# A hybrid decoder trunk on one core: half of the memory's values computed before the output projection, the memory's norm weight moved into the weights' split, other latencies in the order of work

## The chip, the cores and the metric

The kernel runs on one NeuronCore of a Trainium2 chip. The metric is the device time of one execution in microseconds (us). Three runs of the kernel before gave a median of 1250.59 us (1248.96 to 1250.6).

The engines and their short names in the profile: PE (TensorE, matmuls; PEld is its weight loads), ACT (ScalarE), DVE (VectorE), POOL (GpSimd), SP (SyncE, which issues nearly all DMAs here). Each takes its instructions in one fixed order. PE writes into PSUM; ACT and DVE carry results from there to SBUF.

## The reference, cut to what matters

Two layers, 256 tokens, width 1024, all in float32. Each layer is a half-step feed-forward block, a mixer, a cross-attention on 256 memory tokens, and a second half-step feed-forward block:

```
x = x + 0.5 * swiglu(rms_norm(x, ffn1_norm[l]), ...)
x = x + hybrid_mixer(rms_norm(x, mix_norm[l]), w_in[l], ..., w_out[l])
x = x + memory_cross_attention(rms_norm(x, cross_norm[l]), rms_norm(mem, mem_norm[l]),
                               cross_wq[l], cross_wk[l], cross_wv[l], cross_wo[l])
x = x + 0.5 * swiglu(rms_norm(x, ffn2_norm[l]), ...)
...
def memory_cross_attention(h, m, wq, wk, wv, wo):
    q = (h @ wq).reshape(B, S, CROSS_HEADS, CROSS_DH)
    k = (m @ wk).reshape(B, M, CROSS_HEADS, CROSS_DH)
    v = (m @ wv).reshape(B, M, CROSS_HEADS, CROSS_DH)
    ...
```

The keys `m @ wk` and the values `m @ wv` need only the memory, so they can be computed at any time before the attention. `rms_norm(m, w)` is `m / rms(m) * w`, so `rms_norm(m, w) @ W` is `(m / rms(m)) @ (diag(w) W)`: the norm weight may be multiplied into the rows of `W` instead.

The mixer has two groups of heads: HGRN2, a scan over time with a decay (here done as a tree of seven levels), and FoX, causal softmax attention with a forget gate.

## The kernel before, in words

**Products.** Each float32 product is three matmuls on rounded parts: an operand is split into `hi` and `lo`, and `mm3` issues hi·hi, hi·lo and lo·hi (lines L432, L433, L434). Weights come from HBM in slabs of 1 MB (four row blocks of 128 by 512 columns, or two by 1024), in the order of a list `plan`. A slab lands in one of three buffers `raw`; `split_k` makes `whi` (ACT, L140) and `wlo` (DVE, L141), in pieces of 128x1024 with seven buffers each. Where a norm weight is folded into a weight, `split_k` works per row block of 128x512, with a multiplication by a column: ACT L144 and DVE L145. Before the change only the very first feed-forward block does that.

Two forms of product: `xstat` keeps tokens as stationary operand and streams 512 weight columns (matmuls of 128x512), `wstat` keeps weight columns and streams 256 tokens (128x256). Sums go to `acc`, four PSUM tiles in turn; a fifth product waits until the oldest tile is read out. `put_split` (L359 on ACT, then L360 on DVE) does that.

**The order of work** is set by a planner, `drive`: the trunk and the side tasks ("lanes") are generators, which hand over estimated times. A lane yields `(LAT_...,)`, the time that its ACT and DVE work is assumed to take, and until that is over the trunk's matmuls are issued. Within ACT and DVE a scheduler places the instructions, so their order can differ from the code's.

**The mixer** (`mixer`): `xstat` for the scan's values and gate, `wstat` for its forget gates and queries; then the side tasks start: `hgrn` (the scan: `qf`, `kk`, `tots` on DVE, `al` on PE for each level, `ax` and `ho` at its end, `hot` transposes), `memory_task` (loads the memory, L340 squares on ACT, L343 times norm weight and L347 times 1/rms on DVE, then transposes to the features `mf`), `fox_gates`, and two `fox_lane`s of two head pairs each (`fox_stack` makes `fqs` and `fks`; `fs` are the scores, `fpt` the transposed weights, `fpv` the outputs). The trunk meanwhile computes `fq`, `fk`, `fv` (the FoX projections) and the memory's keys `kc` (`wstat` on `mf`, two halves). Then `rows_to_residual` does the output projection: its first matmuls take all four `acc` tiles, and its inputs `oT` come from both groups. The norm of the new residual (`norm_task`) runs beside its end.

**The cross-attention** (`cross`) begins with both halves of the memory's values (`xstat` on `mf`, 48 matmuls of 128x512 each; read out to `vch`, `vcl`), which cover the norm; then queries, scores, and so on.

Of the kernel before, what the change touches and what calls it, by code (L numbers as in the profile page):

```python
# [8 lines left out]
F32 = mybir.dt.float32  # L9
# [8 lines left out]
P = 128  # L18
# [13 lines left out]
HP = 100  # L32
LA_D, LA_S = 3, 1
LAT_NORM, LAT_X = 5.5, 6.5
LAT_LVL, LAT_AX, LAT_HN = 3.0, 1.0, 3.5
LAT_FS, LAT_FT, LAT_CQ, LAT_CS, LAT_CT = 6.0, 2.5, 2.6, 5.6, 3.0
LAT_Q, LAT_G1, LAT_G2, LAT_M = 5.0, 9.0, 2.0, 18.0
LAT_HT = 2.4
LAT_FK = 5.0

OFF_Q, OFF_F, OFF_I, OFF_G = 0, 512, 1024, 1536
OFF_FQ, OFF_FK, OFF_FV = 2048, 2560, 3072
# [3 lines left out]
def hymba_kernel(  # L46
# [43 lines left out]
    def add_cols(w, l, c0, cw, scaled=False):  # L90
        for k0 in range(0, KT, 4):
            plan.append((kview(w, l, c0, cw, k0, 4), 4, cw, k0 if scaled else None))
# [5 lines left out]
    def add_ffn(g, u, d, l, scaled=False):  # L98
        for c0, cw in FCH:
            add_cols(g, l, c0, cw, scaled)  # L100
            add_cols(u, l, c0, cw, scaled)
        add_rows(d, l, FT)

    for l in range(DEPTH):
        add_ffn(ffn1_g, ffn1_u, ffn1_d, l, l == 0)
        for o in (OFF_I, OFF_G, OFF_F, OFF_Q):
            add_cols(w_in, l, o, 512)
        add_cols(w_in, l, OFF_FV + 260, 260)
        add_cols(w_in, l, OFF_FQ, 512)
        add_cols(w_in, l, OFF_FK, 512)  # L110
        add_cols(w_in, l, OFF_FV, 260)
        add_cols(c_wk, l, 0, 512)
        add_cols(c_wk, l, 512, 512)
        add_rows(w_out, l, KT)
        for w in (c_wv, c_wq):
            for c0 in (0, 512):
                add_cols(w, l, c0, 512)
        add_rows(c_wo, l, KT)
        add_ffn(ffn2_g, ffn2_u, ffn2_d, l)

    raws = []
# [13 lines left out]

    def split_k(i, sl, k, hi, lo):

        k0 = plan[i][3]
        if k0 is None:
            nc.scalar.copy(out=hi, in_=sl)  # L140
            nc.vector.tensor_tensor(out=lo, in0=sl, in1=hi.bitcast(F32), op=ALU.subtract)  # L141
        else:
            g = g0[:, k0 + k:k0 + k + 1]
            nc.scalar.mul(hi, sl, g)  # L144
            nc.vector.scalar_tensor_tensor(out=lo, in0=sl, scalar=g, in1=hi.bitcast(F32), op0=ALU.mult,  # L145
                                           op1=ALU.subtract)
# [77 lines left out]
    with in_order():  # L224
        warm_up(14)
        nc.tensor.transpose(g0t[:, 0:8], grow, ident[0:8, 0:8])
        nc.vector.tensor_copy(out=g0, in_=g0t[:, 0:8])
        warm_up(12)
    neghalf = cp.tile([P, 4], F32, name="neghalf")
    nc.vector.memset(neghalf, -0.5)  # L230

    lbr = cp.tile([8, P], F32, name="lbr")

    def consts_mixer():
        it = s4([P, P], I32, "it")
# [626 lines left out]
    def fox_stack(pr, fq, fk, L_, R_, oh):  # L862


        qs = s4([P, 2, 2, S], F32R, "fqs")
        ks = s4([P, 2, 2, S], F32R, "fks")
        for sub in range(2):
            h = 2 * pr + sub
            own = slice(sub * 64, sub * 64 + 64)
            oth = slice(64 - sub * 64, 128 - sub * 64)  # L870
            qv, kv = fq[own, pr, :], fk[own, pr, :]
            nc.scalar.copy(out=qs[own, :, sub, :], in_=qv.unsqueeze(1).to_broadcast([64, 2, S]))  # L872
            nc.scalar.copy(out=ks[own, 0, sub, :], in_=kv)  # L873
# [3 lines left out]
            nc.vector.tensor_tensor(out=ks[own, 1, sub, :], in0=kv, in1=ks[own, 0, sub, :].bitcast(F32),  # L877
                                    op=ALU.subtract)
            nc.vector.tensor_scalar(out=qs[oth, 1, sub, :], in0=L_[oth], scalar1=oh[oth, h:h + 1],
                                    scalar2=None, op0=ALU.mult)  # L880
            nc.gpsimd.tensor_copy(out=ks[oth, 1, sub, :], in_=R_[oth])
# [55 lines left out]
    def mixer(cur, l, consts, nxt_w):  # L937
# [104 lines left out]
    def cross(cur, kc, mf, nxt_w):  # L1042
        f = cur.f
        oT = Feat("cT")
        evs = [Event() for _ in range(4)]
        vc = []

        def head(c, b, qh, ql):
            yield (LAT_CQ,)
# [33 lines left out]
                      po.rearrange("p (k t) -> p k t", k=2))  # L1083
            evs[2 * c + b].fire(1.8)

        for c in range(2):
            vh = s4([P, NT, 512], F32R, "vch")
            vl = s4([P, NT, 512], F32R, "vcl")
            ps = []
            yield from xstat(mf, 512, ps)  # L1090
            for t in range(NT):
                put_split(vh[:, t, :], vl[:, t, :], ps[t])
# [21 lines left out]
    def trunk():  # L1114
        cur = First()
        consts = []

        def early():
            yield (20.0,)
            yield from lower_bounds()  # L1120
            consts.extend(consts_mixer())

        spawn(early())
        for l in range(DEPTH):
            nxt = yield from ffn(cur, mix_norm[l], first=l == 0)
            nxt, kc, mf = yield from mixer(nxt, l, consts, cross_norm[l])
            nxt = yield from cross(nxt, kc, mf, ffn2_norm[l])
# [31 lines left out]
```

## Time and profile before

| | |
|---|---|
| median of three runs | 1250.59 us |
| profiled execution, its time | 1250.42 us |
| its span (first to last instruction) | 1248.6 us |
| mean granted TensorE clock | 0.997 |
| PE busy | 1231.8 us, 99% of the span |
| DVE busy | 767.1 us, 61% |
| ACT busy | 641.2 us, 51% |
| POOL busy | 38.7 us, 3% |
| HBM read | 218.32 MB, 176 GB/s over the span |

The profiled execution took 1.8 us more than its span and lies 0.2 us under the median of the runs. Matmuls overlap in the records (a 128x256 one is recorded as 0.28 us and the next starts 0.12 us after it), so a full PE is read from the starts. The mixer of the first layer lies at about 200 to 356 us, that of the second about 615 us later.

### The profile page before, as it was taken

The numbers are of one execution on the slowest core, as the hardware profiler recorded it, in microseconds if no ns is written. First come the engines' busy times: TensorE is split into PE (matmuls) and PEld (weight loads), VectorE is DVE, ScalarE is ACT, GpSimd is POOL, SyncE is SP. The second block draws the span as 40 slices with busy tenths as digits, with TensorE's granted clock in tenths as the row PEclk, the third lists the DMA queues.
The fourth block names the chain that finished last, engine by engine and source line by source line (L and its number), as shares of the span: only waits on it lengthen the run. The fifth ranks groups of instructions, "written<-read, shape, count | busy, mean of one in ns | idle before, by whom it ended". The sixth has DMA issues, their size and how long they took to land.

```text
span 1248.6 us, 21619 instructions
## 1 busy us (share of the span) xinstructions
PE 1231.8 (99%) x9074; PEld 1126.3 (90%) x9074; DVE 767.1 (61%) x1163; ACT 641.2 (51%) x986; POOL 38.7 (3%) x52
## 2 busy tenths in 40 slices
PE   9999999999999999999999999999999999999997
PEld 7999888989889889998889998889997898999986
DVE  7756547597775675464474464476786766545643
ACT  7555535657754454444354353366585655544532
POOL 0000000002000000000000000000020000000000
PEclk9999999999999999999999999999999999999999
DMA  9555754643453374565474555465442633555640
GB/s 319 178 180 170 239 199 157 219 158 113 169 187 134 102 253 146 192 204 201 135 253 138 200 202 202 135 220 189 147 157 102 248 117 124 177 195 169 236 169 34
DMA packets 100514, 220.76 MB, mean 177 GB/s; under 512 B 4145, under 2 KB 16705, under 8 KB 100417
## 3 DMA queue, kind: packets, MB, share of 16 engines
q1 hardware_dynamic: 100256, 219.11, 51.8%
q8 instruction: 71, 1.16, 0.4%
q10 hardware_dynamic: 160, 0.27, 0.1%
q14 instruction: 27, 0.21, 0.1%
HBM read 218.32 MB, written 1.05 MB: 176 GB/s over the span
## 4 chain that ended last, share of the span: by engine, by line
PE 91%; ACT 5%; DVE 3%; issue 1%; POOL 1%; DMA 0%; POOLq 0%; SPq 0%; ACTq 0%; DVEq 0%
PE acc L432 28%; PE acc L433 28%; PE acc L434 28%; PE pt L353 1%; ACT whi L140 1%; ACT pp L856 1%; ACT fqs L872 1%; DVE wlo L141 1%; PE al L732 1%; ACT fks L874 1%; ACT fks L873 0%; POOL mrs L334 0%; PE cpo L433 0%; DVE mem L343 0%; PE cs L433 0%
## 5 line engine op out<-in xcount | busy, mean ns | idle before, releaser
L141 DVE TENSOR_TENSOR wlo<-raw,whi 128x1024 fp32r<-128x1024 f32 (+1 forms) x356 | 426.3, 1222 | 287.0 <-ACT whi L140 286.0
L140 ACT CAST whi<-raw 128x1024 fp32r<-128x1024 f32 (+1 forms) x356 | 362.8, 1048 | 303.3 <-PE acc L434 152.4
L432 PE MATMUL acc<-xfh,whi 128*128 128x256 f32 x1536 | 434.5, 283 | 0.0
L434 PE MATMUL acc<-xfh,wlo 128*128 128x256 f32 x1536 | 431.0, 281 | 1.9 <-DVE wlo L141 1.9
L433 PE MATMUL acc<-xfl,whi 128*128 128x256 f32 x1536 | 432.0, 281 | 0.0
L434 PEld LDWEIGHTS acc<-xfh,wlo 128*128 128x128 f32 x1536 | 290.2, 189 | 2.1 <-DVE wlo L141 2.1
L433 PEld LDWEIGHTS acc<-xfl,whi 128*128 128x128 f32 x1536 | 290.9, 189 | 0.4
L432 PEld LDWEIGHTS acc<-xfh,whi 128*128 128x128 f32 x1536 | 289.5, 188 | 0.9
L432 PE MATMUL acc<-whi,hth 128*128 128x512 f32 (+1 forms) x352 | 136.4, 388 | 0.0
L433 PE MATMUL acc<-wlo,hth 128*128 128x512 f32 (+1 forms) x352 | 136.3, 387 | 0.0
L434 PE MATMUL acc<-whi,htl 128*128 128x512 f32 (+1 forms) x352 | 135.8, 386 | 0.0
L432 PE MATMUL acc<-whi,xfh 128*128 128x512 f32 (+1 forms) x256 | 95.0, 371 | 0.4 <-ACT xfh L359 0.4
L433 PE MATMUL acc<-wlo,xfh 128*128 128x512 f32 (+1 forms) x256 | 94.0, 367 | 0.0
L434 PE MATMUL acc<-whi,xfl 128*128 128x512 f32 (+1 forms) x256 | 93.6, 366 | 0.1
L434 PEld LDWEIGHTS acc<-whi,htl 128*128 128x128 f32 x352 | 66.2, 188 | 14.5
L432 PEld LDWEIGHTS acc<-whi,hth 128*128 128x128 f32 x352 | 66.1, 188 | 14.4
L433 PEld LDWEIGHTS acc<-wlo,hth 128*128 128x128 f32 x352 | 66.1, 188 | 14.0
L145 DVE SCALAR_TENSOR_TENSOR wlo<-raw,g,whi 128x512 fp32r<-128x512 f32 (+1 forms) x96 | 61.9, 702 | 26.0 <-PE acc L434 18.5
L144 ACT ACTIVATE whi<-raw,g 128x512 fp32r<-128x512 f32 (+1 forms) x96 | 58.2, 678 | 24.5 <-PE acc L433 16.7
L434 PEld LDWEIGHTS acc<-whi,xfl 128*128 128x128 f32 x256 | 48.1, 188 | 8.9 <-DVE xfl L360 0.4
L432 PEld LDWEIGHTS acc<-whi,xfh 128*128 128x128 f32 x256 | 48.1, 188 | 8.8 <-ACT xfh L359 0.6
L433 PEld LDWEIGHTS acc<-wlo,xfh 128*128 128x128 f32 x256 | 48.2, 188 | 8.5 <-DVE wlo L145 0.4
(255 smaller groups left out, 1424.4 us busy)
## 6 DMA issues: line engine op xcount, KB each, us to landing
raw<-in_ffn_w_down_dram SPq DMA_DIRECT2D x44, 1024.0 KB, 4.9
raw<-in_ffn_w_up_dram SPq DMA_DIRECT2D x40, 1024.0 KB, 5.1
raw<-in_ffn_w_gate_dram SPq DMA_DIRECT2D x38, 1024.0 KB, 5.2
raw<-in_w_in_dram SPq DMA_DIRECT2D x24, 1024.0 KB, 5.3
raw<-in_cross_wk_dram SPq DMA_DIRECT2D x8, 1024.0 KB, 5.0
raw<-in_w_out_dram SPq DMA_DIRECT2D x8, 1024.0 KB, 4.8
raw<-in_cross_wv_dram SPq DMA_DIRECT2D x8, 1024.0 KB, 5.3
raw<-in_cross_wq_dram SPq DMA_DIRECT2D x8, 1024.0 KB, 5.6
```

Of the source, the lines that this page charges most:

```text
L140: nc.scalar.copy(out=hi, in_=sl)
L141: nc.vector.tensor_tensor(out=lo, in0=sl, in1=hi.bitcast(F32), op=ALU.subtract)
L144: nc.scalar.mul(hi, sl, g)
L145: nc.vector.scalar_tensor_tensor(out=lo, in0=sl, scalar=g, in1=hi.bitcast(F32), op0=ALU.mult, op1=ALU.subtract)
L353: nc.tensor.transpose(pt[:, j * P:(j + 1) * P], hn[:, kt * P:(kt + 1) * P], ident)
L432: nc.tensor.matmul(ps, lhsT=lh, rhs=rh, start=start, stop=False)
L433: nc.tensor.matmul(ps, lhsT=lh, rhs=rl, start=False, stop=False)
L434: nc.tensor.matmul(ps, lhsT=ll, rhs=rh, start=False, stop=stop)
L732: nc.tensor.matmul(ps[s0:s0 + hb, c0:c0 + hb], lhsT=k[:, h, a:a + hb], rhs=rhs[:, h, a + step:a + step + hb], start=True, stop=True)
L856: nc.scalar.activation(dst, src, AF.Exp, bias=nmx[:, t:t + 1], scale=scale, accum_out=sms[:, t:t + 1])
L872: nc.scalar.copy(out=qs[own, :, sub, :], in_=qv.unsqueeze(1).to_broadcast([64, 2, S]))
L874: nc.scalar.copy(out=ks[oth, 0, sub, :], in_=kv)
```

## The change

Four things change.

1. The first half of the memory's values is computed by a new `memory_values`, called in `mixer` between the keys and the output projection; `cross` computes the second half alone. The slabs in `plan` follow: the first half of `c_wv` comes before `w_out`.
2. The memory's norm weight is no longer multiplied into the memory. It is loaded once for both layers together with `hgrn_lb`, transposed to columns `gcols["mem"]`, and folded into `c_wk` and `c_wv` by the split. The 1/rms is applied by one ACT instruction for each half of the tokens.
3. The assumed latencies of the lanes are longer.
4. In `fox_stack` the POOL copy of `R_` is issued first for each head instead of last.

```diff
-LAT_LVL, LAT_AX, LAT_HN = 3.0, 1.0, 3.5
-LAT_FS, LAT_FT, LAT_CQ, LAT_CS, LAT_CT = 6.0, 2.5, 2.6, 5.6, 3.0
+LAT_LVL, LAT_AX, LAT_HN = 4.0, 1.5, 4.0
+LAT_FS, LAT_FT, LAT_CQ, LAT_CS, LAT_CT = 6.5, 3.5, 2.6, 5.6, 3.0
-LAT_FK = 5.0
+LAT_FK = 6.5
...
-        add_cols(c_wk, l, 0, 512)
-        add_cols(c_wk, l, 512, 512)
+        of_mem = ("mem", 8 * l)
+        add_cols(c_wk, l, 0, 512, of_mem)
+        add_cols(c_wk, l, 512, 512, of_mem)
+        add_cols(c_wv, l, 0, 512, of_mem)
         add_rows(w_out, l, KT)
-        for w in (c_wv, c_wq):
-            for c0 in (0, 512):
-                add_cols(w, l, c0, 512)
+        add_cols(c_wv, l, 512, 512, of_mem)
+        for c0 in (0, 512):
+            add_cols(c_wq, l, c0, 512)
...
-            g = g0[:, k0 + k:k0 + k + 1]
+            g = gcols[gk[0]][:, gk[1] + k:gk[1] + k + 1]
             nc.scalar.mul(hi, sl, g)
...
-        nc.sync.dma_start(out=lbr, in_=hgrn_lb.rearrange("d (h p) -> (d h) p", p=P))
+        nc.sync.dma_start(out=lbr[0:8], in_=hgrn_lb.rearrange("d (h p) -> (d h) p", p=P))
+        nc.sync.dma_start(out=lbr[8:24], in_=mem_norm.rearrange("d (k p) -> (d k) p", p=P))
...
+        gcols["mem"] = small(16, "gmem", bufs=1)
+        nc.vector.tensor_copy(out=gcols["mem"], in_=pt[:, 8:24])
...
             qv, kv = fq[own, pr, :], fk[own, pr, :]
+            nc.gpsimd.tensor_copy(out=ks[oth, 1, sub, :], in_=R_[oth])
...
-            nc.gpsimd.tensor_copy(out=ks[oth, 1, sub, :], in_=R_[oth])
...
-        wmem = load_norm(mem_norm[l])
...
+        vc = []
+        yield from memory_values(mf, vc)
         nxt = Next(nxt_w, lat=LAT_X)
...
                 square(jk, mt, ss, j)
-                gain(mt, mt, wn, j)
             rs = small(1, "mrs")
             inv_rms(ss, rs)
-            apply_norm(mt, rs)
+            nc.scalar.mul(mt, mt, rs)
...
+    def memory_values(mf, vc):
+        ps = []
+        yield from xstat(mf, 512, ps)
+        vh = s4([P, NT, 512], F32R, "vch")
+        vl = s4([P, NT, 512], F32R, "vcl")
+        for t in range(NT):
+            put_split(vh[:, t, :], vl[:, t, :], ps[t])
+        vc.append((vh, vl))
...
-        for c in range(2):
-            vh = s4([P, NT, 512], F32R, "vch")
-            ...
-            vc.append((vh, vl))
+        yield from memory_values(mf, vc)
         yield cur.ev[0]
         yield cur.ev[1]
```

Three places of the order are shown, in the first layer; the second has the same. In the names the number behind the underscore tells tiles of one kind apart. The first is DVE where the scan starts, at about 250 us of the profile before. `mem` rows are the memory's norm, `qf`, `kk` and `tots` the scan, `wlo_2712` (before) and `wlo_2707` (now) the last quarter of the `fq` weights. Before:

```order
L343 TENSOR_TENSOR mem_2555<-mem_2555,wn_2096 128x512
L333 SCALAR_TENSOR_TENSOR ms_2564<-mss_2557 128x1
L723 TENSOR_TENSOR qf_2624<-hq_2404,fg_2272 128x1024
L347 TENSOR_SCALAR mem_2555<-mem_2555,mrs_2563 128x512 x2
L759 TENSOR_TENSOR tots_2660<-fg_2272 128x512
L737 TENSOR_TENSOR Ac_2623<-ad_2626,eye 128x256
L759 TENSOR_TENSOR tots_2660<-tots_2660 128x256
...
L753 TENSOR_TENSOR qf_2624<-qf_2624,fg_2272 128x512
L755 TENSOR_TENSOR kk_2273<-kk_2273,fg_2272 128x512
L766 COPY_PREDICATED Ac_2623<-masks,al_2661 128x256
L141 TENSOR_TENSOR wlo_2712<-raw_2525,whi_2711 128x1024
```

Now:

```order
L340 SCALAR_TENSOR_TENSOR ms_2549<-mss_2544 128x1
L730 TENSOR_TENSOR qf_2619<-hq_2405,fg_2273 128x1024
L766 TENSOR_TENSOR tots_2655<-fg_2273 128x512
L766 TENSOR_TENSOR tots_2655<-tots_2655 128x256
L340 SCALAR_TENSOR_TENSOR ms_2560<-mss_2555 128x1
L766 TENSOR_TENSOR tots_2655<-tots_2655 128x128
...
L144 TENSOR_TENSOR wlo_2707<-raw_2526,whi_2706 128x1024
L990 TENSOR_TENSOR zb_2523<-acc_2524,fb_2097 128x8
...
L760 TENSOR_TENSOR qf_2619<-qf_2619,fg_2273 128x512
L762 TENSOR_TENSOR kk_2274<-kk_2274,fg_2273 128x512
```

The memory's products are gone from this stretch, and the weights' piece has moved from behind the first level of the scan (`qf`, `kk`) to ahead of it. On PE the second level of `al` now stands 39 matmuls of `fq` behind the first, where it was cut in two after 20 and 30.

The second is ACT at the end of the mixer, behind the softmax of the last FoX pairs. `kc_3310` and `kc_3247` are the keys' last half, read out of the fourth `acc` tile; `ppT` are the transposed softmax weights. Before:

```order
L856 ACTIVATE pp_3752,fsm_3758<-pp_3752,fnm_3756 128x256
L140 CAST whi_3818<-raw_3550 128x1024
L140 CAST whi_3890<-raw_3560 128x1024
L359 CAST kc_3310<-acc_3683 128x512
L140 CAST whi_3894<-raw_3560 128x1024
L140 CAST whi_3900<-raw_3812 128x1024
L915 COPY ppT_3838<-fpt_3834 128x384
```

Now:

```order
L863 ACTIVATE pp_3770,fsm_3776<-pp_3770,fnm_3774 128x256
L147 ACTIVATE whi_3831<-raw_3569,gmem_599 128x512 x2
L366 CAST kc_3247<-acc_3698 128x512
L143 CAST whi_3887<-raw_3583 128x1024
L143 CAST whi_3891<-raw_3583 128x1024
L143 CAST whi_3951<-raw_3823 128x1024
L922 COPY ppT_3853<-fpt_3849 128x384
```

The read-out of the keys is two short multiplications behind the softmax instead of two long casts; on PE what follows the keys is now 48 matmuls of the memory's values, in two tiles of `acc` that are long free, and the output projection behind them.

The third is DVE where the first FoX softmax starts, at about 304 us of the profile before. The `ISA` rows find the largest score of each query, and `fnm` is the first number that ACT's exponentials wait for; `hss`, `AX` and `oh` are the scan's output norm. Before:

```order
L901 ISA pp_3418,fmx_3419<-fs_3413,cmask 128x128
...
L901 ISA pp_3436,fmx_3437<-fs_3431,cmask 128x128
L901 ISA fmx_3437 128x1
L905 TENSOR_SCALAR fnm_3422<-fmx_3419 128x2
L901 ISA pp_3436,fmx_3437<-fs_3431,cmask 128x256
```

Now:

```order
L806 TENSOR_SCALAR hss_3354<-hss_3354 128x4
L810 SCALAR_TENSOR_TENSOR AX_3330<-ho_3349,hrs_3360,gw_2100 128x128 x4
L908 ISA pp_3393,fmx_3394<-fs_3388,cmask 128x128
...
L806 TENSOR_SCALAR hss_3376<-hss_3376 128x4
L908 ISA pp_3411,fmx_3412<-fs_3406,cmask 128x128
...
L810 SCALAR_TENSOR_TENSOR oh_3375<-ho_3366,hrs_3382,gw_2100 128x128 x4
L912 TENSOR_SCALAR fnm_3397<-fmx_3394 128x2
```

Before, the scan's norm was over when the first scores came; now the two share DVE.

More of the change, by code (lines that the diff above doesn't have):

```diff
@@ L88, in kview, with add_cols @@
         return w[l, k0 * P:(k0 + nk) * P, c0:c0 + cw].rearrange("(k p) c -> p k c", p=P)
-    def add_cols(w, l, c0, cw, scaled=False):
+    def add_cols(w, l, c0, cw, scaled=None):
         for k0 in range(0, KT, 4):
-            plan.append((kview(w, l, c0, cw, k0, 4), 4, cw, k0 if scaled else None))
+            plan.append((kview(w, l, c0, cw, k0, 4), 4, cw, (scaled[0], scaled[1] + k0) if scaled else None))
     def add_rows(w, l, nkt):
@@ L96, in add_rows, with add_ffn @@
             plan.append((kview(w, l, 0, D, k0, 2), 2, D, None))
-    def add_ffn(g, u, d, l, scaled=False):
+    def add_ffn(g, u, d, l, scaled=None):
         for c0, cw in FCH:
@@ L104, in hymba_kernel @@
     for l in range(DEPTH):
-        add_ffn(ffn1_g, ffn1_u, ffn1_d, l, l == 0)
+        add_ffn(ffn1_g, ffn1_u, ffn1_d, l, ("first", 0) if l == 0 else None)
         for o in (OFF_I, OFF_G, OFF_F, OFF_Q):
@@ L122, in hymba_kernel @@
     pieces = []
+    gcols = {}
     taken = [0]
@@ L136, in split_k @@
     def split_k(i, sl, k, hi, lo):
-        k0 = plan[i][3]
-        if k0 is None:
+        gk = plan[i][3]
+        if gk is None:
             nc.scalar.copy(out=hi, in_=sl)
@@ L227, in hymba_kernel @@
         nc.vector.tensor_copy(out=g0, in_=g0t[:, 0:8])
+        gcols["first"] = g0
         warm_up(12)
@@ L230, in hymba_kernel @@
     nc.vector.memset(neghalf, -0.5)
-    lbr = cp.tile([8, P], F32, name="lbr")
+    lbr = cp.tile([24, P], F32, name="lbr")
     def consts_mixer():
@@ L298, in lower_bounds @@
     def lower_bounds():
-        nc.sync.dma_start(out=lbr, in_=hgrn_lb.rearrange("d (h p) -> (d h) p", p=P))
+        nc.sync.dma_start(out=lbr[0:8], in_=hgrn_lb.rearrange("d (h p) -> (d h) p", p=P))
+        nc.sync.dma_start(out=lbr[8:24], in_=mem_norm.rearrange("d (k p) -> (d k) p", p=P))
         yield (6.0,)
         pt = smp("lbt")
-        nc.tensor.transpose(pt[:, 0:8], lbr, ident[0:8, 0:8])
+        nc.tensor.transpose(pt[:, 0:24], lbr, ident[0:24, 0:24])
         yield 0.1
+        gcols["mem"] = small(16, "gmem", bufs=1)
+        nc.vector.tensor_copy(out=gcols["mem"], in_=pt[:, 8:24])
         a = small(8, "lba")
@@ L977, in mixer @@
         mf = Feat("mf")
-        spawn(memory_task(l, wmem, mf, ev_m))
+        spawn(memory_task(mf, ev_m))
         fv = s4([P, NT, 512], F32, "fv")
@@ L1014, in mixer, with memory_task @@
         yield from rows_to_residual(act, KT, 1.0, TAIL, nxt, lambda kt: ev_h if kt < 4 else ev_p[kt - 4])
-        return nxt, kc, mf
-    def memory_task(l, wn, mf, ev):
+        return nxt, kc, vc, mf
+    def memory_task(mf, ev):
         mf.alloc(0)
@@ L1039, in memory_task, with cross @@
         ev.fire(1.6)
-    def cross(cur, kc, mf, nxt_w):
+    def memory_values(mf, vc):
[6 more added lines that the diff above has]
+        vc.append((vh, vl))
+    def cross(cur, kc, vc, mf, nxt_w):
         f = cur.f
@@ L1045, in cross @@
         evs = [Event() for _ in range(4)]
-        vc = []
         def head(c, b, qh, ql):
@@ L1084, in head @@
             evs[2 * c + b].fire(1.8)
-        for c in range(2):
-            vh = s4([P, NT, 512], F32R, "vch")
[L1088 to L1092, printed above, removed]
-            vc.append((vh, vl))
+        yield from memory_values(mf, vc)
         yield cur.ev[0]
@@ L1125, in trunk @@
             nxt = yield from ffn(cur, mix_norm[l], first=l == 0)
-            nxt, kc, mf = yield from mixer(nxt, l, consts, cross_norm[l])
-            nxt = yield from cross(nxt, kc, mf, ffn2_norm[l])
+            nxt, kc, vc, mf = yield from mixer(nxt, l, consts, cross_norm[l])
+            nxt = yield from cross(nxt, kc, vc, mf, ffn2_norm[l])
             cur = yield from ffn(nxt, ffn1_norm[l + 1] if l + 1 < DEPTH else final_norm, l + 1 == DEPTH)
```

## The prediction

> **What bounds the kernel now.** I read the page's busy times first, then PE's list of waits, then the rows around each wait, and last the busy times by stretch.
>
> ```profile
> PE 1231.8 (99%) x9074; PEld 1126.3 (90%) x9074; DVE 767.1 (61%) x1163; ACT 641.2 (51%) x986; POOL 38.7 (3%) x52
> PE acc L432 <- DVE kc L360: 2.9, 2, 1.5
> PE acc L434 <- DVE wlo L141: 1.9, 2, 1.0
> ...
> PE al L732 <- DVE kk L755: 0.8, 2, 0.6
> PE fpv L925 <- ACT ppT L915: 0.7, 2, 0.4
> PE fs L894 <- DVE fks L877: 0.6, 4, 0.2
> ```
>
> PE is the bound, and what is left to gain is small: the five waits that lie in the mixer (`kc`, `wlo`, `kk`, `ppT`, `fks`) come to 2.9 + 1.9 + 0.8 + 0.7 + 0.6 = 6.9 us over both layers. What else the list has lies almost all at the start of the kernel and stays. The change takes no matmul away and adds none of weight, so it can only act on these waits, or make new ones. Where a new one could come is told by the stretches of the first mixer (columns: window; its length; busy us, with counts, of PE, PEld, DVE, ACT, POOL; clock; DMA share; GB/s):
>
> ```profile
> 262.00:282.00 20.00, 20.00 (x369) 18.88 (x367) 16.86 (x30) 12.21 (x20) 0.00 (x0) 1.00 0.55 183
> 282.00:297.00 15.00, 15.00 (x130) 14.99 (x129) 10.32 (x19) 10.05 (x28) 4.69 (x7) 1.00 0.39 142
> 297.00:316.00 19.00, 18.62 (x164) 18.04 (x163) 16.21 (x51) 17.75 (x42) 2.34 (x4) 1.00 0.27 92
> 316.00:333.00 17.00, 15.24 (x112) 14.15 (x112) 15.86 (x52) 14.61 (x39) 0.00 (x0) 1.00 0.29 96
> ```
>
> From 297 to 333 us, where both FoX lanes run beside the keys, ACT is busy for 32.4 of 36 us and DVE for 32.1. There is little cover: what an instruction waits for there depends on its place in the queue.
>
> **Part by part. First, the keys' read-out** (the largest wait). These are PE's rows at the start of the output projection, in which `fpt` is a lane's transposes, and what ACT and DVE did before:
>
> ```profile
> 330.18 0.82 PE L912 MATMUL fpt<-ident,pp 128*128 128x128 f32 x6
> 332.44 0.51 PE L432 MATMUL acc<-whi,oTh 128*128 128x512 f32 x1 [1.45 <-DVE kc L360]
> 333.24 0.82 PE L912 MATMUL fpt<-ident,pp 128*128 128x128 f32 x6
> 333.81 0.47 PE L432 MATMUL acc<-whi,oTh 128*128 128x512 f32 x1
> ...
> 328.36 1.99 ACT L140 CAST whi<-raw 128x1024 fp32r<-128x1024 f32 x2
> 329.43 2.36 DVE L141 TENSOR_TENSOR wlo<-raw,whi 128x1024 fp32r<-128x1024 f32 x2 [0.19 <-ACT whi L140]
> 331.71 0.68 DVE L360 TENSOR_TENSOR kc<-acc,kc 128x512 fp32r<-128x512 f32 x1
> ```
>
> The keys' last product needed 1.99 + 0.6 us on ACT and 2.36 + 0.68 on DVE before its PSUM tile came free; the projection's fourth tile waited for it. The same six transposes without a wait are followed after 333.81 - 333.24 = 0.57 us, here after 2.26, so PE lost 1.7 us, 3.4 in both layers (the list, which counts from the modelled end of the matmul, has 2.9). In the new order 48 matmuls of 128x512 come between, in tiles read out long before. At 0.23 us each (the starts of the rows at 366.98 and 367.21, shown below) they give 11 us of cover: gain 3.4. What is late next are the values' own two tiles, which the projection takes as its third and fourth: needed six and nine matmuls (1.4 and 2.1 us) behind the values' end, and ready, with an ACT copy of 0.6 and a DVE subtraction of 0.68 each, about 0.7 and 1.4 us behind it, if no long cast stands ahead; the last cast ahead waits for a weights' buffer that comes free 2.8 us before the end. I cost this at nothing.
>
> **Second, the scan's start.** PE's rows, one stretch of each layer:
>
> ```profile
> 255.98 0.28 PE L433 MATMUL acc<-xfl,whi 128*128 128x256 f32 x1
> 256.43 0.50 PE L732 MATMUL al<-qf,kk 128*32 128x32 f32 x34 [0.17 <-DVE kk L755]
> 257.89 0.39 PE L434 MATMUL acc<-xfh,wlo 128*128 128x256 f32 x1 [0.96 <-DVE wlo L141]
> ...
> 870.02 0.28 PE L433 MATMUL acc<-xfl,whi 128*128 128x256 f32 x1
> 870.91 0.50 PE L732 MATMUL al<-qf,kk 128*32 128x32 f32 x34 [0.62 <-DVE kk L755]
> 872.38 0.39 PE L434 MATMUL acc<-xfh,wlo 128*128 128x256 f32 x1 [0.96 <-DVE wlo L141]
> ...
> L343 DVE TENSOR_TENSOR mem<-mem,wn 128x512 f32<-128x512 f32 x8 | 5.4, 683 | 0.0
> L347 DVE TENSOR_SCALAR mem<-mem,mrs 128x512 f32<-128x512 f32 x8 | 3.5, 484 | 1.8 <-POOL mrs L334 1.8
> L334 POOL TENSOR_TENSOR mrs<-ms,neghalf 128x1 f32<-128x1 f32 x4 | 4.8, 1196 | 88.7 <-DVE ms L333 88.7
> ```
>
> A matmul and half a level of `al` take 0.12 + 0.5 us; the rows show 1.91 and 2.36, a loss of 1.3 + 1.7 = 3.0 us. Two edits meet here. The memory's products leave DVE: per layer 4 x 0.683 + 4 x 0.484 = 4.7 us, and 0.9 of waiting for POOL. And the order puts the weights' piece ahead of the scan's first level, and 39 matmuls (4.7 us) between the levels. The new DVE queue, from the end of the previous `wlo` at 248.0: `qf` 1.2, `tots` 1.9, then the piece 1.2, so done by about 253 us, while PE wants it at about 255.9. On ACT the two new multiplications of 128x1024 wait for POOL's `mrs` (1.2 us), and the cast `whi_2706` stands behind the first: about 252. The margin is nearly 3 us, and I count the whole 3.0 as gained. The price of such a multiplication is not in the trace; it lies between 1.05 (the cast of that size) and 1.28 us (two scaled pieces, below).
>
> **Third, the two small waits.** `LAT_FT` puts 24 matmuls instead of 15 between `fpt` and `fpv` (2.9 instead of 1.8 us), and in ACT's queue the `ppT` copies stand ahead of the casts; `LAT_FK` puts 51 instead of 36 matmuls before the second `fs`, 1.8 us more for a wait of 0.3 per layer. Gain 0.7 + 0.6 = 1.3, by the list. The POOL copy issued first matters little: it reads `R_` alone.
>
> Together 3.4 + 3.0 + 1.3 = 7.7 us.
>
> **Fourth, what the scaled split costs.** One slab in each form, from the first feed-forward block:
>
> ```profile
> 44.93 2.57 ACT L144 ACTIVATE whi<-raw,g 128x512 fp32r<-128x512 f32 x4 [2.82 <-PE acc L433]
> 45.69 2.74 DVE L145 SCALAR_TENSOR_TENSOR wlo<-raw,g,whi 128x512 fp32r<-128x512 f32 x4 [0.81 <-ACT whi L144]
> L872 ACT CAST fqs<-fq 64x512 fp32r<-64x512 f32 x16 | 10.0, 622 | 0.3
> L873 ACT CAST fks<-fk 64x256 fp32r<-64x256 f32 x16 | 6.5, 404 | 0.0
> ```
>
> Against 1.99 and 2.36 us for the plain form, a slab costs ACT 0.58 and DVE 0.38 us more; with eight slabs a layer that is 4.6 and 3.0 us. PE pays only where a queue is late. The tightest place I find is the scan's last product `ho`: its operand `AX` is copied by ACT behind 12 scaled pieces (7.7 us), nine FoX copies (3 x 0.62 + 6 x 0.40 = 4.3) and six copies out of PSUM or into `A` (some 3 us, an estimate from the 0.40 to 0.62 of copies of like size). With four copies into `A` ahead (1.6) and about 2 us until they can start, that is some 19 us from the fifth level on, while PE covers it with 132 matmuls and three small groups, 132 x 0.12 + 2.5 plus a tenth or two for each change of shape: 19. That is nothing to spare; I take 0 here, and the bounds are 0 and 1 us per layer.
>
> **Fifth, two waits that the new order makes.**
>
> ```profile
> 293.98 1.12 DVE L803 SCALAR_TENSOR_TENSOR oh<-ho,hrs,gw 128x128 f32<-128x128 f32 x4 [1.13 <-POOL hrs L801]
> 304.09 0.28 PE L432 MATMUL acc<-mfh,whi 128*128 128x256 f32 x1
> 304.21 0.28 PE L433 MATMUL acc<-mfl,whi 128*128 128x256 f32 x1
> 310.59 0.55 DVE L860 TENSOR_SCALAR pp<-pp,frc 128x128 f32<-128x128 f32 x2
> 365.88 1.03 PE L353 MATMUL pt<-ident,hn 128*128 128x128 f32 x8
> 366.98 0.40 PE L433 MATMUL acc<-wlo,mfh 128*128 128x512 f32 x1
> 367.21 0.40 PE L434 MATMUL acc<-whi,mfl 128*128 128x512 f32 x1
> 367.71 1.28 DVE L360 TENSOR_TENSOR xfl<-pt,xfh 128x512 fp32r<-128x512 f32 x2
> ```
>
> Matmuls of 128x256 start 0.12 us apart, those of 128x512 0.23. The first softmax took 311.14 - 304.09 = 7.05 us from where PE leaves the scores to the end of DVE's last product. In the new order the scan's norm shares DVE with it: four products (1.1 us) and a wait for POOL (1.1) stand ahead of the first `fnm`. PE covers 48 matmuls and three groups of transposes, 5.8 + 2 = 7.8 us. With 1.1 us added the last transposes wait about 0.4 us per layer (bounds 0 and 1.5, with POOL's wait paid in full). At the start of the cross-attention the second set of `xf` is ready at 367.71 + 0.68 = 368.4; of the matmuls of 128x512 behind the transposes (366.98 is the second), six are left, so the first matmul on `xf` would start at 366.98 + 5 x 0.23 = 368.1 and the second, which reads this set, at 368.2: 0.2 us per layer (bounds 0 and 0.7, one read-out more). Together 0.8 + 0.4 = 1.2 us.
>
> The rest is small: one DMA of 16 short rows and a copy of 16 columns more, two loads of a norm weight fewer, on queues that nothing here waits for.
>
> **The sum.** 1250.4 - 7.7 + 1.2 = 1243.9 us, against the profiled execution's own time, which lies 0.2 us under the median.
>
> **Rivals.** (a) The waits come back in part: ACT and DVE, full for 36 us, pass their 4.6 and 3.0 us on where I took 0. With 1 us at `ho` and 0.75 more at the softmax in each layer, 3.5 us are lost again: 1247.4.
>
> (b) Nothing in sum: the lanes' slack only moves from wait to wait, as the waits of 0.2 to 0.6 us at many places suggest; 1249 to 1252. Against it: the largest, `kc`, is removed by 11 us of cover.
>
> (c) Slower: ACT becomes the bound at `ho`. Each microsecond that the `AX` copy is late beyond the 19 us above stops PE for one, in both layers. It decides from (6.5 + 2.5) / 2 = 4.5 us per layer on: the scaled pieces would have to take 1.0 us instead of 0.64, or a slab's DMA to hold ACT that long. Time then 1253 or more. Against it: the first block's rows show four pieces in 2.57 us.
>
> (d) POOL's copies against the splits. Beside DVE's `wlo` a copy took much longer than alone:
>
> ```profile
> L881 POOL CAST fks<-R x16: 393/399/1349, 294.0 to 919.7; 64x256 fp32r<-64x256 f32 x16
> ```
>
> If each of the eight copies per layer, now issued among the scan's and the splits' work, held DVE for its 0.4 us and PE paid half, 2 x 8 x 0.4 / 2 = 3.2 us come back: 1247.1. I doubt it, since nothing waited for POOL there. The Trainium skill, "SBUF — State Buffer", section "Who interferes with whom", has a rule that speaks for it: a DVE instruction with two SBUF inputs contends with a GpSimd instruction that reads SBUF, and the later one is blocked in full. By that rule the trace's 1.35 us copies are blocked ones, which agrees; whether DVE was held in turn, no row here shows. By the rule the sum would be 1247.1, by the rows 1243.9.
>
> **Chances.** My sum 0.60 (its own range 1241.3 to 1246.5: with no new wait and what PE loses beyond the list at the small waits too, or with the upper bounds at one place); (a) 0.13; (d) 0.05; (b) 0.14; (c) 0.08. A measurement of this kernel tells a change from none beyond about 0.2%, 2.5 us, so under 1248.1 us counts as faster: 0.78; same 0.14; slower 0.08. The range takes in (a) and (d) and part of (b): 1241 to 1249.5.
>
> **What would show it.** In the list of PE's waits `kc` and the splits' `wlo` should be gone from the mixer, `ppT` and `fks` nearly; a wait of `fpt` for DVE `pp`, and one of `acc` for `xfl`, a few tenths each, should be there. `ho` waiting for ACT `AX` shows (a) or (c). I would be wrong if the values' tiles `vcl` came late, since nothing but DVE's order covers them, or if the memory's multiplication on ACT, held up by `mrs`, made the casts behind it late for `fq`.

## The result and the profile after

The changed kernel takes 1242.62 us in the median of four runs (1242.16 to 1242.67), the kernel before 1249.89 us on the same chip; the ratio is 0.9941, 95% interval 0.9928 to 0.9953. The forecast of 1243.9 us and its sign hold. The runs of the kernels without part 2, the one before among them, fall into two groups some 1.4 us apart (22 of 83 in the upper; of the kernel before two of each here, near 1249.1 and 1250.5 us, the profiled one in the upper), which leaves about 0.7 us of doubt in the gain of 7.3. The profiled execution's span went from 1248.6 to 1240.8 us, by 7.8.

First the page's busy times, then PE's list of waits, of the changed kernel (us in total, times, longest). Between the two kernels the line numbers shift by 7 where the code is the same:

```profile
PE 1227.8 (99%) x9074; PEld 1122.9 (90%) x9074; DVE 767.1 (62%) x1180; ACT 653.6 (53%) x1022; POOL 36.9 (3%) x52
PE fs L901 <- DVE AX L810: 2.1, 2, 1.1
PE warm L223 <- POOL ident masks.py:199: 1.4, 1, 1.4
PE pt L501 <- DVE hn L494: 1.0, 1, 1.0
PE acc L439 <- ACT xfh L366: 0.6, 1, 0.6
PE al L739 <- issue: 0.5, 1, 0.5
PE fpt L919 <- DVE oTl L367: 0.3, 2, 0.2
```

All five waits that the prediction wanted gone are gone: `kc`, the splits' `wlo`, `kk`, `ppT`, `fks`. In their place stands a wait that it did not have: the scores `fs` for DVE's `AX`, once in each layer. The rows around it, PE and then DVE, in the first layer:

```profile
297.82 1.17 PE L901 MATMUL fs<-fks,fqs 128*128 128x128 f32 x8
300.04 1.28 PE L901 MATMUL fs<-fks,fqs 128*128 128x128 f32 x8 [1.06 <-DVE AX L810]
301.16 0.28 PE L439 MATMUL acc<-mfh,whi 128*128 128x256 f32 x1
297.49 0.17 DVE L806 TENSOR_SCALAR hss<-hss 128x4 f32<-128x4 f32 x1 [1.25 <-ACT AX L804]
298.86 1.12 DVE L810 SCALAR_TENSOR_TENSOR AX<-ho,hrs,gw 128x128 f32<-128x128 f32 x4 [1.20 <-POOL hrs L808]
299.90 0.28 DVE L908 CUSTOM_DVE_ANT_0 pp<-fs,cmask 128x128 f32<-128x128 f32 x1
301.75 1.13 DVE L810 SCALAR_TENSOR_TENSOR oh<-ho,hrs,gw 128x128 f32<-128x128 f32 x4 [0.93 <-POOL hrs L808]
```

The second eight score products start 1.12 us before the next row, the first eight 2.22 before the second: PE lost 1.1 us, 2.2 in both layers. `fs` computes nothing from `AX`. What the two share is PSUM: everything that isn't `acc` takes one of four tiles (`pss`, `bufs=4`). `ho` takes two of them, the first two `fs` tiles the other two (eight of the sixteen products), and the third `fs` tile is that of the first `ho`, which `AX<-ho` is still reading. The tiles are not taken strictly in turn. If they were, the fourth `fs` tile would be that of the second `ho`; but `oh<-ho` reads that one only from 301.75 us on, and all sixteen products have begun before 301.16. The fourth starts at about 300.6, right behind the end of the softmax's reading of the first `fs` tile (300.5), so it most likely took that one, the tile that came free next.

The other places that the prediction named:

```profile
307.36 0.82 PE L919 MATMUL fpt<-ident,pp 128*128 128x128 f32 x6
308.25 0.28 PE L441 MATMUL acc<-mfh,wlo 128*128 128x256 f32 x1
308.69 1.15 PE L919 MATMUL fpt<-ident,pp 128*128 128x128 f32 x6 [0.16 <-DVE oTl L367]
309.59 0.37 PE L439 MATMUL acc<-mfh,whi 128*128 128x256 f32 x1
329.73 1.47 PE L919 MATMUL fpt<-ident,pp 128*128 128x128 f32 x12
330.96 0.48 PE L439 MATMUL acc<-whi,mfh 128*128 128x512 f32 x1
376.37 0.40 PE L439 MATMUL acc<-xfh,whi 128*128 128x256 f32 x2
376.89 0.39 PE L440 MATMUL acc<-xfl,whi 128*128 128x256 f32 x1
L1038 ACT ACTIVATE mem<-mem,mrs 128x1024 f32<-128x1024 f32 x4 | 4.6, 1153 | 2.4 <-POOL mrs L341 2.4
```

Where PE stood still for the keys' read-out, twelve transposes now run into the values' matmuls in 1.23 us. The softmax wait is there (0.3 us before the second `fpt` group and 0.3 inside it), but for `oTl`, which reads the tile of `hot`: the four tiles again. At the start of the cross-attention two matmuls take 0.52 instead of 0.24 us.

### The profile page after: what moved, and what is told of

Same layout as the page of the kernel before. It is cut to its first block, busy times and chain, and to the rows that moved or that the text cites. A ratio compares the mean times of both kernels' runs of the same rounds, so it can differ in the third digit from the quotient of the medians.

```text
span 1240.8 us, 21619 instructions
## 1 busy us (share of the span) xinstructions
PE 1227.8 (99%) x9074; PEld 1122.9 (90%) x9074; DVE 767.1 (62%) x1180; ACT 653.6 (53%) x1022; POOL 36.9 (3%) x52
## 3 DMA queue, kind: packets, MB, share of 16 engines
HBM read 217.28 MB, written 1.05 MB: 176 GB/s over the span
## 4 chain that ended last, share of the span: by engine, by line
PE 93%; DVE 3%; ACT 1%; POOL 1%; issue 1%; DMA 0%; POOLq 0%; SPq 0%; DVEq 0%; ACTq 0%
PE acc L439 29%; PE acc L440 29%; PE acc L441 29%; PE pt L360 1%; DVE wlo L144 1%; PE al L739 1%; DVE wlo L148 1%; ACT whi L147 0%; POOL rs L341 0%; POOL hrs L808 0%; PE cpo L440 0%; DVE pp L867 0%; PE cs L440 0%; PE cs L439 0%; PE cs L441 0%
## 5 line engine op out<-in xcount | busy, mean ns | idle before, releaser
L144 DVE TENSOR_TENSOR wlo<-raw,whi 128x1024 fp32r<-128x1024 f32 (+1 forms) x324 | 389.1, 1223 | 275.4 <-ACT whi L143 274.4
L143 ACT CAST whi<-raw 128x1024 fp32r<-128x1024 f32 (+1 forms) x324 | 330.4, 1048 | 276.1 <-PE acc L441 137.1
```

## The experiments

Each ran in five rounds beside the kernel before, 1249.1 to 1249.4 us there in the median. Where the text says "of the same rounds", the two kernels ran side by side on one chip.

**The parts alone and the parts left out.** The parts are numbered as in the change. Alone, with all else as before: part 1 (`a_only`), part 2 (`b_only`), part 3 (`c_only`). One left out of the changed kernel: `no_a`, `no_b`, `no_c` (and `no_d` for the POOL copy). The cores of the edits against the changed kernel:

```diff
# no_a
-        yield from memory_values(mf, vc)     # in mixer, ahead of the output projection
+        yield from memory_values(mf, vc)     # a second time in cross
# no_b
-            nc.scalar.mul(mt, mt, rs)
+            apply_norm(mt, rs)
...
+                gain(mt, mt, wn, j)
# no_c
-LAT_LVL, LAT_AX, LAT_HN = 4.0, 1.5, 4.0
+LAT_LVL, LAT_AX, LAT_HN = 3.0, 1.0, 3.5
...
-LAT_FK = 6.5
+LAT_FK = 5.0
```

`a_only`: 

> The kernel before with part 1 of the change alone: the first half of the memory's values ahead of the output projection. First theory (each of PE's waits belongs to one part): the wait for the keys' read-out goes (3.4 us over both layers), a wait for xf of about 0.4 comes at the cross-attention, the waits for wlo, kk, ppT and fks stay as they were: 1247 us. Rival (the latencies carry the gain, since they re-space all lanes): no gain, 1249 to 1251 us.

`b_only`: 

> The kernel before with part 2 alone: the memory's norm weight in the split of the weights. First theory: DVE's queue at the scan's start is freed, so PE's waits for wlo and kk go (3.0 us); the waits for kc, ppT and fks stay; the scaled split costs at most 1 us: 1247 to 1248 us. Rival: the extra 4.6 us of ACT and 3.0 us of DVE work per layer eat it, since the lanes run at the same spacing: 1250 to 1252 us.

`c_only`: 

> The kernel before with part 3 alone: the longer latencies. First theory: the latencies alone lose: the two small waits for ppT and fks go (1.3 us), but fs waits for the scan's output to be read out of PSUM (2.4 us) and fpt for the scan's transposes (some 1 us), and the waits for kc and wlo stay: 1251 to 1253 us. Rival (the latencies carry the gain): 1244 to 1246 us.

`no_c`: 

> The changed kernel with the old latencies (parts 1, 2 and 4). First theory: the two waits that the new latencies make (fs on DVE AX 2.4 us, fpt on DVE oTl about 1.2 us, by starts) go, the two small ones for ppT and fks come back (1.3 us): faster than the changed kernel by some 2 us, 1240 to 1241 us. Rival (the latencies carry the gain): 1247 to 1249 us.

`no_a`: 

> The changed kernel without part 1: both halves of the values are computed in the cross-attention, as before; the rest as changed. My theory of the sum (the keys' read-out cost 3.4 us, the values' early half pays 0.4 to 0.6 of it back at the start of the cross-attention): the wait of acc for DVE kc is in PE's list again with 2.5 to 3, 1245.2 to 1246.2. Rival (the parts work only together, as the latencies and the folded norm weight did): no more than 0.2% from the kernel before, 1247.5 to 1249.

`no_b`: 

> The changed kernel without part 2: the memory is again multiplied by its norm weight and by 1/rms on DVE, and the weights are split plainly. With the values early alone 1246.2 and the latencies alone 0.8 us faster than before, a plain sum of the two is 1245.4 us: wlo (1.9) and kk (0.8) stand in PE's list at the scan's start, kc, ppT and fks are gone, fs waits for AX as in the changed kernel (2.1). Rival (the longer latencies pay only where part 2 has taken DVE's work away): no better than the values early alone, 1246.2 to 1247. Other rival (the folded norm is worth nothing by itself and in sum): 1242.6 to 1243.6, as the changed kernel.

Measured, with the waits of PE's list that matter:

| kernel | median, us | ratio, 95% interval | waits (us, both layers) |
|---|---|---|---|
| `a_only` | 1246.18 | 0.9974 (0.9964 to 0.9984) | wlo 1.9, kk 1.0, ppT 0.8, fks 0.6 |
| `b_only` | 1248.77 | 0.9994 (0.9985 to 1.0003) | kc 2.8, kk 2.1, ppT 1.3, fks 0.6 |
| `c_only` | 1248.42 | 0.9992 (0.9983 to 1.0001) | kc 2.6, fs for AX 2.1, wlo 1.9, kk 0.8 |
| `no_c` (parts 1, 2, 4) | 1247.6 | 0.9985 (0.9976 to 0.9993) | ppT 2.4, kk 1.9, fks 0.5 |
| `no_a` (2, 3, 4) | 1245.43 | 0.9967 (0.9955 to 0.9979) | kc 3.3, fs for AX 2.1, fpt for oTl 0.3 |
| `no_b` (1, 3, 4) | 1245.98 | 0.9973 (0.9963 to 0.9984) | fs for AX 2.1, wlo 1.9, kk 0.8, fpt for oTl 0.3 |
| all | 1242.62 | 0.9941 (0.9928 to 0.9953) | fs for AX 2.1, fpt for oTl 0.3 |

Part 1 is worth 3.0 us alone and about 3.5 beside the others (`no_a` stands 3.7 under its before, the whole 7.3, and `no_a` is 3.4 slower than `no_d` of the same rounds, which is the changed kernel but for part 4): as expected. Part 2 is worth 0.4 alone, within what can be told from nothing, and about 4 us beside parts 1 and 3; part 3 is worth 0.8 alone, nothing to speak of beside part 1 (3.4 against 3.0), and 5.7 beside parts 1 and 2. Parts 2 and 3 work only together: the two without part 1 (`no_a`) are worth 3.7. Part 2 beside part 1 alone even costs: `no_c` is 1.4 us slower than `a_only` of the same rounds. `no_c` was to be 1240 to 1241 and came out at 1247.6, my largest miss, and `c_only`, costed as a loss by one theory and as a clear gain by the other, was neither.

The rows of `no_c` show why. PE and DVE at the scan's second level:

```profile
257.48 0.76 PE L739 MATMUL al<-qf,kk 128*32 128x32 f32 x64
262.60 0.76 PE L739 MATMUL al<-qf,kk 128*32 128x32 f32 x64 [0.62 <-DVE kk L762]
260.12 1.22 DVE L144 TENSOR_TENSOR wlo<-raw,whi 128x1024 fp32r<-128x1024 f32 x1
261.26 0.68 DVE L760 TENSOR_TENSOR qf<-qf,tots 128x512 f32<-128x512 f32 x1
261.86 0.68 DVE L762 TENSOR_TENSOR kk<-kk,tots 128x512 f32<-128x512 f32 x1
```

And the same of the changed kernel:

```profile
258.92 0.76 PE L739 MATMUL al<-qf,kk 128*32 128x32 f32 x64
264.90 0.76 PE L739 MATMUL al<-qf,kk 128*32 128x32 f32 x64
260.49 1.22 DVE L144 TENSOR_TENSOR wlo<-raw,whi 128x1024 fp32r<-128x1024 f32 x1
261.62 0.68 DVE L760 TENSOR_TENSOR qf<-qf,tots 128x512 f32<-128x512 f32 x1
262.22 0.68 DVE L762 TENSOR_TENSOR kk<-kk,tots 128x512 f32<-128x512 f32 x1
```

DVE does the same in both, and `kk` is ready at about 262.5 and 262.9 us. PE wants it 5.1 us after the first level's start with the old latencies (less the wait, 4.5), 6.0 with the new. Part 2 takes the stall for `wlo` away and with it the time in which DVE caught up; without more matmuls between the levels the wait goes to the next level. At `ppT` ACT's queue decides. Its rows in `no_c`:

```profile
310.00 1.94 ACT L147 ACTIVATE whi<-raw,gmem 128x512 fp32r<-128x512 f32 x3
311.84 0.56 ACT L366 CAST kc<-acc 128x512 fp32r<-128x512 f32 x1
312.30 0.85 ACT L922 COPY ppT<-fpt 128x384 f32<-128x384 f32 x2
313.04 1.95 ACT L147 ACTIVATE whi<-raw,gmem 128x512 fp32r<-128x512 f32 x3
314.89 0.84 ACT L922 COPY ppT<-fpt 128x384 f32<-128x384 f32 x2
```

Six scaled pieces, 3.9 us, stand ahead of the last `ppT` copies, and `fpv` waits 1.2 us in each layer.

**Is it `LAT_FT` that covers `ppT`?**

```diff
-LAT_FS, LAT_FT, LAT_CQ, LAT_CS, LAT_CT = 6.5, 3.5, 2.6, 5.6, 3.0
+LAT_FS, LAT_FT, LAT_CQ, LAT_CS, LAT_CT = 6.5, 2.5, 2.6, 5.6, 3.0
```

> The changed kernel with LAT_FT 2.5, as before the change, and all else as changed: 15 instead of 24 matmuls between fpt and fpv, 1.1 us less cover. Theory (part 2 puts scaled pieces on ACT, 0.58 us a slab more, and the ppT copies are late by them; LAT_FT covers that): fpv waits for ACT ppT with 0.8 to 1.2 us per layer, as it did with all latencies as before (2.4 in the list): 1244.2 to 1245.0 us. Rival (what covered ppT was the changed place of fs and of the scan's end, not LAT_FT): no ppT wait, 1242 to 1243.

Measured 1242.08 us, 0.9939 (0.9927 to 0.995), no `ppT` wait. My theory fell, the rival holds: 15 matmuls are enough. ACT's rows in this kernel, at the same `fpt`:

```profile
308.11 0.85 ACT L922 COPY ppT<-fpt 128x384 f32<-128x384 f32 x2
308.85 0.73 ACT L147 ACTIVATE whi<-raw,gmem 128x512 fp32r<-128x512 f32 x1
309.48 0.89 ACT L922 COPY ppT<-fpt 128x384 f32<-128x384 f32 x2
```

One scaled piece stands there instead of six. The other new latencies move the FoX lane against the weights' slabs, and with it the place of the pieces in ACT's queue. Which of them does it was not tried.

**Does POOL's copy matter (part 4)?**

```diff
-            nc.gpsimd.tensor_copy(out=ks[oth, 1, sub, :], in_=R_[oth])
...
+            nc.gpsimd.tensor_copy(out=ks[oth, 1, sub, :], in_=R_[oth])
```

> The changed kernel with POOL's copy of R_ issued last for each head, as before. Mine: it reads R_ alone, nothing waits for POOL there, 1242.0 to 1243.2, no difference that can be measured. Rival (d) of the prediction, that POOL's copies among the splits hold DVE: if this place of the copies costs, the kernel without it is 1 to 3 us faster, 1239.5 to 1241.5. Third: the copy is late as the last one, as fks was before, and the wait of fs for fks is back with 0.3 per layer: 1243.2 to 1244.

Measured 1242.02 us, 0.994 (0.9927 to 0.9952): no difference, as costed. `fs` waits for `AX` as before (2.1), the wait of `fpt` is not in the list.

**Is it the PSUM tile?** ACT copies `ho` out of PSUM first, and the norm works on the copy.

```diff
-            pv = po.rearrange("p (h e) -> p h e", h=4)
+            ov = sm.tile([P, 512], F32, name=nm("hov"), tag="hov", bufs=2)
+            nc.scalar.copy(out=ov, in_=po)
+            pv = ov.rearrange("p (h e) -> p h e", h=4)
```

> The changed kernel, with ho copied by ACT from PSUM to a new SBUF tile before the scan's norm reads it; PE's order is the same. Theory T1 (the third score product fs of lane 1 waits for a PSUM tile that DVE's product AX, L810, still reads, 1.06 us per layer by the list, 1.2 by the starts): the tile is free about 0.6 us after ho ends, the wait of fs for DVE AX is gone from PE's list, and 2 to 2.4 us of it come back, less what four more ACT copies (2 per layer, some 0.6 us each) do to the softmax behind them, 0 to 1.2: 1240.2 to 1242.0 us. Rival T2 (the wait is for the whole DVE queue, and only the name in the list is the tile's): another wait of about 1 us per layer stands in the same place, 1242 to 1244.

Measured 1245.32 us, 0.9965 (0.9953 to 0.9978): 2.7 us slower than the changed kernel, and 3.3 slower than `no_d` of the same rounds. PE, and the DVE and POOL rows beside it:

```profile
297.43 2.10 PE L903 MATMUL fs<-fks,fqs 128*128 128x128 f32 x16
301.88 0.60 PE L818 MATMUL hot<-ident,AX 128*128 128x128 f32 x4
304.54 0.66 PE L818 MATMUL hot<-ident,oh 128*128 128x128 f32 x4 [2.06 <-DVE fmx L910]
302.13 1.94 DVE L812 SCALAR_TENSOR_TENSOR oh<-hov,hrs,gw 128x128 f32<-128x128 f32 x4 [0.93 <-POOL hrs L810]
304.07 0.41 DVE L910 CUSTOM_DVE_ANT_0 pp<-fs,cmask 128x256 f32<-128x256 f32 x1
302.16 1.77 POOL L881 CAST fks<-R 64x256 fp32r<-64x256 f32 x4
```

The tile was the cause: the sixteen `fs` now run in one piece. But T1's time was wrong, since the next taker of the same four tiles waits. The second `hot` tile is that of the second `fs`, and the trace names its last reader: the score maximum `fmx`, taken by the row at 304.07 us, which stands behind the four `oh` products in DVE's queue. `hot` waits 2.1 us for it in each layer. The two ACT copies (0.6 us each) and slower `oh` products made it later: in the changed kernel `oh` takes 1.13 us, here 1.94. Behind the wait of the second layer the granted clock also falls to half for 3.4 us (917.6 to 921.0), which costs about 1.4 us more (an estimate: some 15 matmuls start 0.21 instead of 0.12 us apart); the last section shows another such stretch. So T2 is right as far as DVE's queue goes, and wrong that the tile was only a name.

**The scan's end earlier.** `LAT_LVL` 3.5: 33 matmuls between levels.

```diff
-LAT_LVL, LAT_AX, LAT_HN = 4.0, 1.5, 4.0
+LAT_LVL, LAT_AX, LAT_HN = 3.5, 1.5, 4.0
```

> The changed kernel with LAT_LVL 3.5 instead of 4.0: 33 instead of 39 matmuls between the levels of the scan, so that its end comes some 30 matmuls earlier and the norm of ho is over before the first scores. T1 (the longer level time bought the cover of kk at the scan's start, and paid with the collision of the scan's norm and the first softmax): the wait of fs for AX (2.1 in the list) and that of fpt for oTl (0.2) are gone; 33 matmuls give 0.7 us per level less cover than 39, so kk comes back with 0 to 0.7 us per layer: 1239.5 to 1241.5. Rival (39 matmuls are needed, since the second level of al reads what DVE has ready only 4.5 us after the first): kk back with 1 us per layer and more, fs as before elsewhere: 1242.5 to 1245.

Measured 1244.59 us, 0.9961 (0.9949 to 0.9974). The list:

```profile
PE fpt L919 <- DVE pp L867: 3.1, 2, 1.6
PE fs L901 <- DVE oTl L367: 1.2, 2, 0.6
PE al L739 <- DVE kk L762: 0.6, 1, 0.6
```

The wait for `AX` is gone and `kk` is back with 0.6 us in one layer, both as T1 had it. It did not foresee that `fs` then meets the next reader of the four tiles, `hot`'s `oTl`, and that the second pairs' `fpt` comes too early for their softmax.

**The scores 15 matmuls later.** `LAT_FK` longer by 1.5 us for the first pairs alone (`fk15`), and the same with POOL's copy as before (`fk15_d`).

```diff
+FK1 = 1.5
...
-            yield (LAT_FK,)
+            yield (LAT_FK + (FK1 if pr < 2 else 0.0),)
```

> The changed kernel with 1.5 us more of LAT_FK for the first pairs alone: 15 matmuls (1.8 us) stand between ho and the scores fs, so that ho's PSUM tile is read out by AX before fs wants it; hot follows 6 matmuls behind fs instead of 21, at nearly the same time. T1 (PE waits for the tile, and the matmuls put there are work that is done anyway): the fs wait (2.1 by the list, 2.4 by starts) is gone; hot needs oh, whose end at 302.9 us hung on the second hss behind the score maxima on DVE, so 0 to 0.5 us per layer may come back there, and the same again at fpt: 1240.2 to 1241.8. Rival T2 (the chain hss, POOL's hrs, oh on DVE is what bounds, as it was when ho was copied out first, and PE only meets it elsewhere): hot waits 1 us per layer and more, 1242.2 to 1244.

> The same with POOL's copy of R_ issued last for each head, as before the change. Without the 1.5 us that order gave 0.6 us less than the changed kernel, inside what can be told. If that was real (four copies of 0.44 in a row on POOL stand ahead of nothing, but the fpt wait of 0.3 was gone with it): 0.3 to 0.8 us under its neighbour of this call. If it was the spread of the runs: the same within 0.3 us. If POOL's copies now land on fks' DVE subtractions: an fs wait for fks and 0.5 us more.

Measured 1240.91 us, 0.9928 (0.9915 to 0.9941), the median of five runs from 1240.47 to 1241.08 (a sixth, 2012.55 us at a granted clock of 0.556, is left out), and 1241.19 us, 0.9931 (0.9919 to 0.9943). The POOL copy's place again makes no difference. Rows of `fk15`:

```profile
299.25 1.55 PE L902 MATMUL fs<-fks,fqs 128*128 128x128 f32 x12
301.93 0.73 PE L902 MATMUL fs<-fks,fqs 128*128 128x128 f32 x4 [1.14 <-DVE oh L811]
299.47 0.16 DVE L807 TENSOR_SCALAR hss<-hss 128x4 f32<-128x4 f32 x1
300.75 1.13 DVE L811 SCALAR_TENSOR_TENSOR oh<-ho,hrs,gw 128x128 f32<-128x128 f32 x4 [1.13 <-POOL hrs L809]
```

The time is as T1 gave it, the way only half. The third tile comes free in time, and now the fourth, that of the second `ho`, holds PE until `oh` has read it, 1.14 us by the list. What is gained is that the `fpt` waits are gone. This version is the best of all: 8.5 us under before on its chip, where the changed kernel was 7.3 under on its own. That is 1.2 us between them, less than these two measurements can tell. `ft25`, the changed kernel with a shorter `LAT_FT`, is also 1.2 us slower than `fk15`, of the same rounds, and its runs (1241.61 to 1242.68) do not overlap with those of `fk15`.

## Why the prediction was right, and where it was wrong

- **The keys' read-out, 3.4 us:** right. The wait is gone, `a_only` gained 3.0, and taking the part out cost 3.4 to 3.6. The values' tiles `vcl` were not late.
- **The scan's start, 3.0 us:** right in sum, but the step gave the gain to the memory's products leaving DVE. `b_only` shows that alone moving the waits: `wlo` gone, `kk` up from 0.8 to 2.1, `ppT` up from 0.7 to 1.3. The margin of nearly 3 us that I worked out holds for `wlo` only; the second level's `kk` is covered by the 39 matmuls, which I named and did not cost by themselves.
- **The small waits, 1.3 us:** gone, but I put `ppT` down to 24 instead of 15 matmuls, and `ft25` shows that 15 do. What I also named, the place of the copies in ACT's queue, is what the runs show. By the starts of PE's rows these two waits had cost about 2.6 us in both layers rather than the list's 1.3.
- **Scaled pieces at `ho`, 0 (bounds 0 and 1):** right. No wait for ACT's `AX` copy is in the list; rivals (a) and (c) at that place did not show. The multiplication of 128x1024, bounded at 1.05 to 1.28 us, takes 1.153.
- **Softmax, 0.4 us per layer:** about 0.6, inside the bounds, but the operand is `oTl` and not `pp`. Start of the cross-attention, 0.2: measured 0.28.
- **The term that was missing:** `fs` for the tile that `AX` reads, 2.2 us in both layers. I saw the scan's norm meet the first softmax on DVE, and priced it as a delay of `fnm`; I did not count the four PSUM tiles that the two also share, although I did so for `acc`.

The costs are thus 2.2 + 1.3 + 0.6 = 4.1 us instead of 1.2, and the gains 7.8 + 4.1 = 11.9 instead of 7.7. Of the 4.2 us more, 1.3 are the small waits by the starts. Another 1.4 are a stretch of half clock in the second layer of the profile before (last section), which the prediction did not notice. By the starts of the same matmuls the changed kernel gains 3.1 us in the first layer and 5.1 in the second, and it loses 0.4 ahead of the first mixer, which is not in this sum. The remaining 1.5 lie in smaller pieces, such as the cut level of `al` and other changes of shape, which I have not resolved. That the forecast of 1243.9 came so near 1242.6 is partly luck: costs and gains were both put too small, by 2.9 and 4.2 us.

Rival (d), POOL against DVE, was rightly given little here: taking POOL's copies to their old place changed nothing. Its mechanism is real all the same, below.

## What to carry to other kernels

Where PE is full, a part that removes a wait and one that lengthens the distance to the next need can each be worth nothing alone and several microseconds together; test parts by leaving them out as well as alone. Before two lanes are moved side by side, count the PSUM tiles that they share and who reads each last: a matmul can wait for a product that it has nothing to do with. Taking one tile's wait away, by a copy or by an earlier or later start, moved the wait to the next taker in all three trials here, as the readers' queue (DVE's norm and softmax) stayed as long. Compare the same stretch in several profiles: one stretch of half clock in the profile before looked like part of the gain.

## What the runs showed of the hardware

**POOL beside DVE.** `oh`'s product takes 344 ns when `ho` is read from PSUM, with POOL's copies beside it in the changed kernel, and 542 ns in `sb_ho`, where both its inputs are in SBUF, while `AX` from the same places, with POOL idle, takes 348. POOL's copies were as long in both (557 ns mean):

```profile
L810 DVE SCALAR_TENSOR_TENSOR oh<-ho,hrs,gw 128x128 f32<-128x128 f32 x8 | 2.3, 344 | 1.9 <-POOL hrs L808 1.9
L812 DVE SCALAR_TENSOR_TENSOR oh<-hov,hrs,gw 128x128 f32<-128x128 f32 x8 | 3.9, 542 | 1.9 <-POOL hrs L810 1.9
L812 DVE SCALAR_TENSOR_TENSOR AX<-hov,hrs,gw 128x128 f32<-128x128 f32 x8 | 2.3, 348 | 2.4 <-POOL hrs L810 2.4
```

That is 4 x (0.542 - 0.344) = 0.8 us per layer more, beside 1.77 us of POOL's copies. That is what the prediction left open ("whether DVE was held in turn, no row here shows"). The Trainium skill, "SBUF — State Buffer", section "Who interferes with whom", says that a DVE instruction with two SBUF inputs contends with a GpSimd instruction that reads SBUF, and that one with at most one SBUF input, outside the modes that use both ports, does not; these three rows agree.

**A stretch of half clock.** In the profile before, the granted TensorE clock is 0.5 from 873.5 to 876.9 us, right behind the second layer's waits for `kk` and `wlo`, and matmuls of 128x256 start 0.21 us apart there instead of 0.12. `a_only` has the same code and the same two waits at that place, 1.4 us earlier, and no such stretch. The stretch alone, then the same place in both, before and `a_only` (columns as in the prediction):

```profile
873.50:876.90 3.40, 3.40 (x44) 3.11 (x44) 3.37 (x8) 0.22 (x1) 0.00 (x0) 0.50 0.90 223
873.00:877.00 4.00, 4.00 (x49) 3.71 (x49) 3.97 (x9) 0.22 (x1) 0.00 (x0) 0.57 0.80 200
871.60:875.60 4.00, 4.00 (x62) 3.82 (x61) 4.00 (x9) 0.63 (x2) 0.00 (x0) 1.00 0.75 191
```

In the same 4 us PE gets through 49 matmuls instead of 62, and from there on the kernel before is 1.4 us further behind. Between its first and its last microseconds only `sb_ho`'s profile has another such stretch, of the same 3.4 us, behind a wait of 2.1. That only the kernels without part 2 have two groups of runs fits a stretch behind the waits that part 2 removes, but one trace alone shows it there. That the waits bring it on is not shown: the same waits in `a_only`, and the 2.1 us of `hot` in `sb_ho`'s first layer, were not followed by one.
